# Sums of the FFN's down weights: from VectorE to accumulating transfers in DRAM

## The chip, the core and the metric

The kernel runs on one core of a Trainium2 chip. The core has five engines with queues of their own: TensorE (PE, matrix products, with its weight loads shown as PEld), VectorE (DVE), ScalarE (ACT), GpSimd (POOL) and SyncE (SP). Transfers between DRAM and on-chip memory are issued from the queues of SP, ACT and POOL and are carried out by 16 DMA engines that all queues share. The metric is the device time of one execution in microseconds (us); lower is better.

## The reference

The program computes two layers of a decoder trunk on 512 tokens of width 1024, in float32. Each layer normalises its input, projects it once into four parallel branches (a gated short convolution, a sparse attention with a top-k selection, a gated linear recurrence, a cross-attention into 256 memory tokens), lifts and gates the branches, sums them, projects and adds the residual. Then comes the feed-forward part (FFN), and only that is touched here:

```python
hf = rmsnorm(x, norm_ffn)
gate, up = jnp.split(hf @ ffn_w_up, 2, axis=-1)
return x + (jax.nn.silu(gate) * up) @ ffn_w_down      # ffn_w_down: 2816 x 1024 per layer
```

## The kernel before

Every product of float32 matrices is made of three products of rounded halves: an operand is split into `hi` and `lo`, and hi·hi, hi·lo and lo·hi are summed (`mm3`, lines 275 to 277). Weights come in through `wchunk` (line 219, on SP's queue) into one of two `w_raw` buffers of 1 MB; ACT writes the rounded half `w_hi` (through the helper at line 97) and DVE the rest `w_lo` (line 230), each into one of three buffers of half a chunk (`W_BUFS`).

A layer is first `mixer`, with the projections, the selection, the attention and the recurrence (`head`, whose first steps on DVE are the subtractions at line 911 and the scan at line 918, which reads `chunk_mult`, set by POOL at line 873), then `ffn`. In the middle of the mixer `values` makes the recurrence's values `hv` (line 688). The residual goes through a DRAM tensor, `x_spill`, written by eight stores at line 1030 and read again by POOL's transfers at line 1202 or 1207.

The FFN works in parts of four to six pairs of 128-row blocks of its hidden width. For each pair the up and gate products are made, then `operands` forms the left operands. The down product of a part is not made directly: `down` uses a scheme with seven block products in place of eight. With the weight block pair of index i cut into b11, b12, b21, b22 (row block first, column half second), it needs the sums

    t1 = b12 - b11,  t2 = b22 - t1,  t3 = b22 - b12,  t4 = b21 - t2

of the right operand, and like sums of the left one. `weight_sums` (lines 1084 to 1094) makes them one pair at a time: POOL loads 1 MB (line 1087), DVE makes four subtractions (lines 1090 to 1093), and POOL stores the four sums into the DRAM tensor `w_sums` (line 1094). The call for the next pair follows each pair's operands. `down` later loads them from there on SP's queue (lines 1151 and 1176). The loaded tile `w_raw7` of `weight_sums` is one buffer that the loads of `down` (every third of them, `raw_tile`) and of `x_in` use too. The last two pairs of layer 0 go without sums (`plain`, `add_down`). `evict` (line 1255) adds each finished product to the accumulator `acc`.

The order of the instructions on each engine is not that of the text. A planner (the framework's scheduler, which runs the program against its own model of times) takes for each engine, among the instructions whose inputs and buffers are free, the one of the highest priority, which is the earliest in the text if no priority is given. It puts in the semaphores, for on-chip tiles and for DRAM tensors. A manual dependency of kind NoSync only orders; one of kind Sync makes the instruction wait.

Of the kernel before, what the change touches and what calls it, by code (L numbers as in the profile page):

```python
# [12 lines left out]
F32 = mybir.dt.float32  # L13
# [4 lines left out]
OP = mybir.AluOpType  # L18
# [3 lines left out]
P = 128  # L22
# [47 lines left out]
def hybrid_trunk(ctx: ExitStack, tc: tile.TileContext, x, mem, positions, norm_mix, w_in, conv_w,  # L70
                 dsa_q_norm, dsa_k_norm, hgrn_lower_bounds, hgrn_out_norm, mem_norm, mem_w_kv,
                 mem_q_norm, mem_k_norm, w_lift, w_out, norm_ffn, ffn_w_up, ffn_w_down, out):
    nc = tc.nc
    act, dve, pe, pool = nc.scalar, nc.vector, nc.tensor, nc.gpsimd
# [8 lines left out]
    sp = start.enter_context(tc.tile_pool(name="start", bufs=1))  # L83

    order = mybir.DependencyInfo(mybir.DependencyClass.NoSync, mybir.DependencyReason.DATA)
    tables = {AF.Exp: "natural_log_exp_and_others", AF.Ln: "natural_log_exp_and_others",
              AF.Silu: "silu_and_others"}
    table = {"set": None, "load": None, "users": []}
# [14 lines left out]
    def mm_ps():  # L103
        return pmm.tile([P, 512], F32, name="mm")
# [4 lines left out]
    def tr_ps():  # L109
        return pat.tile([P, 512], F32, name="tr", bufs=TR_BUFS)  # L110

    def f(ap):
        return ap.bitcast(F32)
# [29 lines left out]
    ps = tr_ps()  # L143
    for _ in range(WARM):
        pe.matmul(ps[:, :P], ones_d, ones_d, start=True, stop=True)
    rows = sp.tile([P, P], F32, name="rows")
# [13 lines left out]
    ps = tr_ps()  # L160
# [80 lines left out]
    def wchunk(src, kt, n):  # L241
        return Chunk(src, kt, n)
# [19 lines left out]
    def tokens_wide(ws, a, kt, pss):  # L262

        k0 = 0
        for w in ws:
            for ks, _, _ in w.parts:
                for t, ps in enumerate(pss):
                    for k in ks:
                        mm3(ps, pair(a, k0 + k, slice(t * P, (t + 1) * P)), w.at(k), k0 + k == 0, k0 + k == kt - 1)
            k0 += w.kt  # L270
# [9 lines left out]
    wt_dram = nc.dram_tensor("w_sums", [DEPTH, P, FF // 256, 4, 512], F32, kind="Internal").ap()  # L280
    kv_dram = [nc.dram_tensor(f"kv{l}", [P, 4, 2, 2, MEM], F32, kind="Internal").ap() for l in range(DEPTH)]

    def new_h():
        return (state.tile([P, KD, S], F32R, name="h_hi", bufs=1),
                state.tile([P, KD, S], F32R, name="h_lo", bufs=1))
# [230 lines left out]
    def mixer(l, h, norms, cm):  # L516
# [165 lines left out]
        def values(hv):  # L682
            ws = [wchunk(w_in[l][k0 * P:(k0 + 4) * P, C_GI:C_GI + 512], 4, 512) for k0 in (0, 4)]
            pss = [mm_ps() for _ in range(MM_BUFS)] + [tr_ps()]
            tokens_wide(ws, h, KD, pss)
            for t, ps in enumerate(pss):
                with tc.high_priority(offset=AHEAD):
                    i = A(hv[:, t, :], ps, AF.Copy, scale=r_t[:, t:t + 1])
                if t < MM_BUFS:
                    behind.append(i)  # L690
            yield

        with pool_("dsa") as dp:
# [365 lines left out]
    HALF = S // 2  # L1059
    A11, A12, A22, S2, S1, S4, S3 = range(7)  # L1060
    C1, C2 = slice(512, 1024), slice(0, 512)
# [19 lines left out]

    SUM3, SUM1, SUM2, SUM4 = range(4)

    def weight_sums(fp, l, i):

        raw = fp.tile([P, 4, 512], F32, name="w_raw7")
        nc.gpsimd.dma_start(raw.rearrange("p (e c) n -> p e (c n)", e=2),
                            ffn_w_down[l][2 * i * P:2 * (i + 1) * P, :].rearrange("(e p) n -> p e n", p=P))
        b12, b11, b22, b21 = (raw[:, j, :] for j in range(4))
        dve.tensor_sub(b11, b12, b11)  # L1090
        dve.tensor_sub(b12, b22, b12)
        dve.tensor_sub(b22, b22, b11)
        dve.tensor_sub(b21, b21, b22)
        nc.gpsimd.dma_start(wt_dram[l, :, i], raw)

    def operands(fp, g0, g1, plain, n_ops):

        hi, lo = (fp.tile([P, 7, HALF], F32R, name=nm, bufs=n_ops) for nm in ("a_hi", "a_lo"))
        if plain:
            for o, g in ((0, g0), (2, g1)):  # L1100
                h_, l_ = (x[:, o:o + 2, :].rearrange("p a b -> p (a b)") for x in (hi, lo))
                A(h_, g, AF.Copy)
                dve.tensor_sub(l_, g, f(h_))
            return hi, lo

        def put(o, n, src):
            h_, l_ = (x[:, o:o + n, :].rearrange("p a b -> p (a b)") for x in (hi, lo))
            A(h_, src, AF.Copy)
            dve.tensor_sub(l_, src, f(h_))

        put(A11, 1, g0[:, :HALF])
        put(A12, 2, g1)
        dve.tensor_add(g0[:, HALF:], g0[:, HALF:], g1[:, HALF:])
        dve.tensor_sub(g0[:, :HALF], g0[:, HALF:], g0[:, :HALF])
        both = g1.rearrange("p (a b) -> p a b", b=HALF)
        dve.tensor_sub(both, both, g0[:, None, :HALF].to_broadcast([P, 2, HALF]))
        put(S2, 2, g0)
        put(S4, 2, g1)
        return hi, lo
# [73 lines left out]
    def ffn(l, h, ssq):  # L1193
        r_b = norm_feature(ssq)
        last = l == DEPTH - 1
        n_f = FF // 256
        parts = ((0, 6, False), (6, n_f, False)) if last else ((0, 5, False), (5, 9, False), (9, n_f, True))

        with tc.tile_pool(name="ffn", bufs=1, reuse_waits="tile") as fp:
            def x_chunk(m):  # L1200
                xc = fp.tile([P, S], F32, name="x_c", bufs=4)
                nc.gpsimd.dma_start(xc, x_dram[:, m, :])
                return xc

            def x_in(m0):
                xs = fp.tile([P, 2048], F32, name="w_raw7")
                nc.gpsimd.dma_start(xs.rearrange("p (m t) -> p m t", t=S), x_dram[:, m0:m0 + 4, :])
                for m in range(4):
                    ps = tr_ps()
                    for t in range(NT):  # L1210
                        pe.transpose(ps[:, t * P:(t + 1) * P], xs[:, m * S + t * P:m * S + (t + 1) * P], ident)
                    A(acc[:, :, (m0 + m) * P:(m0 + m + 1) * P], ps.rearrange("p (a b) -> p a b", b=P), AF.Copy)

            acc = None
            for part, (f0, f1, plain) in enumerate(parts):
                ops = []
                if not plain:
                    weight_sums(fp, l, f0)
                for fc in range(f0, f1):
                    wg = wchunk(ffn_w_up[l][:, fc * 256:(fc + 1) * 256], KD, 256)  # L1220
                    wu = wchunk(ffn_w_up[l][:, FF + fc * 256:FF + (fc + 1) * 256], KD, 256)
                    gs = [fp.tile([P, S], F32, name="fg", bufs=3) for _ in range(2)]
                    us = [fp.tile([P, S], F32, name="fu", bufs=2) for _ in range(2)]
                    for w, dsts in ((wg, gs), (wu, us)):
                        for dst, ps in zip(dsts, features(w, h, (0, 1))):
                            dve.tensor_mul(dst, ps, r_b)
                    for g, u in zip(gs, us):
                        A(g, g, AF.Silu)
                        dve.tensor_mul(g, g, u)  # L1229
                    ops.append(operands(fp, *gs, plain, 6 if last else 5))  # L1230
                    if acc is None:
                        acc = fp.tile([P, NT, D], F32, name="acc")
                        if not last:
                            pool.memset(acc, 0.0)
                    if last and fc in (1, 3):
                        x_in(2 * fc - 2)
                    if not plain and fc + 1 < f1:
                        weight_sums(fp, l, fc + 1)
                final = last and part == len(parts) - 1
                wd = ffn_w_down[l][f0 * 256:f1 * 256, :]  # L1240
                if plain:
                    h2, ssq2 = new_h(), new_ssq()
                    add_down(x_chunk, wd, [Pairs(t) for t in zip(*ops)], 2 * len(ops), acc, h2, ssq2,
                             lambda c: g_mix(l + 1, c))
                    return h2, ssq2

                def evict(bank, t0, cols, done=False, tail=False):
                    tail = final and tail
                    adds = []
                    with tc.high_priority(offset=2 * AHEAD):  # L1250
                        for t, ps in enumerate(bank):
                            for w in (slice(0, 256), slice(256, 512)) if tail else (slice(0, 512),):
                                c = slice(cols.start + w.start, cols.start + w.stop)
                                d = acc[:, t0 + t, c]
                                adds.append(dve.tensor_add(d, d, ps[:, w]))  # L1255
                                if final and done:
                                    q = nc.scalar if tail and w.start else nc.sync if t0 or tail else nc.gpsimd
                                    q.dma_start(out[0][(t0 + t) * P:(t0 + t + 1) * P, c], d)
                    return adds

                down(fp, wd, wt_dram[l, :, f0:f1], ops, evict)
        return None, None

# [33 lines left out]
```

## Time and profile before

| | |
|---|---|
| median of 3 runs | 2032.3 us (2030.45 to 2032.67) |
| the profiled execution | 2033.14 us, span 2031.4 us |
| PE busy | 2015.5 us, 99% of the span |
| DVE busy | 1427.8 us, 70% |
| ACT busy | 1067.9 us, 53% |
| POOL busy | 45.0 us, 2% |
| DMA queue of POOL | 46.80 MB, 6.2% of 16 engines' span |
| DMA queue of SP | 208.51 MB, 32.0% |

The profile is of one execution. In a row of instructions, `out<-in` names the tiles, then partitions x elements, a count, and times. A wait is put down to the instruction that ended it. PE's rows overlap, since matmuls are pipelined: a matmul of 512 columns is shown as 0.39 us, and starts 0.23 us after the one before it. `q1` is SP's DMA queue, `q0` POOL's, `q10` ACT's.

### The profile page before, as it was taken

What the parts mean: (1) busy time and instruction counts of PE and PEld (TensorE: products, weight loads), DVE (VectorE), ACT (ScalarE), POOL (GpSimd) and SP (SyncE); (2) the same over time, 40 slices, a digit from 0 to 9 for tenths busy, and PEclk for the clock granted to TensorE, in tenths of its full rate; (3) what the DMA queues carried; (4) which work ended last, traced back from release to release, by engine and by line L of the source; (5) the groups of instructions that cost most, each with busy time, mean ns of one, the idle gap of its engine ahead of it and who ended that gap; (6) DMA issues with size and microseconds to landing.
All of it is one profiled execution on the core that took longest, in us unless ns stands there. A gap on an engine that the chain in (4) does not pass through costs nothing.

```text
span 2031.4 us, 26667 instructions
## 1 busy us (share of the span) xinstructions
PE 2015.5 (99%) x10100; PEld 1691.8 (83%) x10100; DVE 1427.8 (70%) x2774; ACT 1067.9 (53%) x1914; POOL 45.0 (2%) x86
## 2 busy tenths in 40 slices
PE   9999999999999999999999999999999999999999
PEld 8998987778888888888889898877888788888887
DVE  5768897647776576666556889955678566666666
ACT  7653654766566433333345455477667544333333
POOL 0000000000000000000000000000000000000000
PEclk9999999999999999999999999999999999999999
DMA  7623232222233554663352223232222445566644
GB/s 252 214 88 104 68 104 62 78 69 83 83 110 123 196 213 150 227 232 128 108 182 71 92 79 94 73 94 67 80 79 80 152 140 192 186 212 217 225 150 155
DMA packets 192160, 269.86 MB, mean 133 GB/s; under 512 B 5775, under 2 KB 157921, under 8 KB 189089
## 3 DMA queue, kind: packets, MB, share of 16 engines
q1 hardware_dynamic: 176320, 208.51, 32.0%
q0 software_dynamic: 9568, 46.80, 6.2%
q10 hardware_dynamic: 6144, 12.87, 1.7%
q8 instruction: 79, 1.29, 0.3%
q14 instruction: 49, 0.39, 0.1%
HBM read 232.50 MB, written 35.65 MB: 132 GB/s over the span
## 4 chain that ended last, share of the span: by engine, by line
PE 95%; DVE 2%; DMA 2%; ACT 1%; issue 0%; DVEq 0%; SPq 0%; ACTq 0%
PE mm L275 28%; PE mm L277 27%; PE mm L276 27%; PE tr L732 1%; PE at L702 1%; PE tr L726 1%; PE at L703 1%; PE at L277 1%; PE at L276 1%; PE at L275 1%; DVE acc L1255 1%; PE tr L275 1%; PE tr L277 1%; PE tr L276 1%; DMA w_raw<-in_ffn_w_down_dram 1%; ACT w_hi L97 0%
## 5 line engine op out<-in xcount | busy, mean ns | idle before, releaser
L275 PE MATMUL mm<-h_hi,w_hi 128*128 128x512 f32 x1664 | 651.3, 393 | 1.4 <-ACT w_hi L97 0.7
L276 PE MATMUL mm<-h_lo,w_hi 128*128 128x512 f32 x1664 | 652.4, 392 | 0.0
L277 PE MATMUL mm<-h_hi,w_lo 128*128 128x512 f32 x1664 | 648.4, 392 | 0.6 <-DVE w_lo L230 0.5
L97 ACT ACTIVATE w_hi<-w_raw 128x1024 fp32r<-128x1024 f32 (+1 forms) x384 | 394.9, 1033 | 391.5 <-PE mm L276 248.5
L230 DVE TENSOR_TENSOR w_lo<-w_raw,w_hi 128x1024 fp32r<-128x1024 f32 x304 | 369.4, 1218 | 203.9 <-ACT w_hi L97 202.8
L275 PEld LDWEIGHTS mm<-h_hi,w_hi 128*128 128x128 f32 x1664 | 313.2, 188 | 67.2 <-ACT w_hi L97 1.8
L277 PEld LDWEIGHTS mm<-h_hi,w_lo 128*128 128x128 f32 x1664 | 312.8, 188 | 65.5 <-DVE w_lo L230 1.4
L276 PEld LDWEIGHTS mm<-h_lo,w_hi 128*128 128x128 f32 x1664 | 313.1, 188 | 63.8 <-issue 0.6
L1079 DVE TENSOR_TENSOR w_lo<-w_raw,w_hi 128x1024 fp32r<-128x1024 f32 (+1 forms) x80 | 86.4, 1090 | 64.9 <-ACT w_hi L97 64.8
L277 PE MATMUL mm<-w_hi,h_lo 128*128 128x256 f32 (+2 forms) x368 | 109.3, 297 | 0.0
L276 PE MATMUL mm<-w_lo,h_hi 128*128 128x256 f32 (+2 forms) x368 | 109.1, 297 | 0.0
L275 PE MATMUL mm<-w_hi,h_hi 128*128 128x256 f32 (+2 forms) x368 | 108.7, 298 | 0.0
L97 ACT ACTIVATE a_hi<-fg 128x512 fp32r<-128x512 f32 (+1 forms) x84 | 48.5, 580 | 109.1 <-DVE fg L1229 81.8
L275 PE MATMUL mm<-y_hi,w_hi 128*128 128x512 f32 x256 | 100.3, 394 | 1.2 <-ACT y_hi L97 1.2
L276 PE MATMUL mm<-y_lo,w_hi 128*128 128x512 f32 x256 | 100.5, 393 | 0.0
L277 PE MATMUL mm<-y_hi,w_lo 128*128 128x512 f32 x256 | 100.2, 392 | 0.0
L97 ACT ACTIVATE prob<-prob,small 128x256 f32<-128x256 f32 (+3 forms) x128 | 68.9, 555 | 16.7 <-DVE small L715 9.0
L276 PEld LDWEIGHTS mm<-w_lo,h_hi 128*128 128x128 f32 x368 | 70.1, 191 | 2.2
L277 PEld LDWEIGHTS mm<-w_hi,h_lo 128*128 128x128 f32 x368 | 70.0, 191 | 1.9
L275 PEld LDWEIGHTS mm<-w_hi,h_hi 128*128 128x128 f32 x368 | 69.8, 191 | 1.9
L97 ACT ACTIVATE gate_e<-gate 128x512 f32<-128x512 f32 x64 | 40.2, 628 | 45.2 <-DVE gate L534 44.6
L276 PE MATMUL mm<-w_lo,a_hi 128*128 128x512 f32 x160 | 62.2, 389 | 0.0
(404 smaller groups left out, 3301.3 us busy)
## 6 DMA issues: line engine op xcount, KB each, us to landing
w_raw<-in_w_in_dram SPq DMA_DIRECT2D x72, 1024.0 KB, 5.3
w_raw<-in_ffn_w_up_dram SPq DMA_DIRECT2D x44, 1024.0 KB, 5.3
w_raw<-in_ffn_w_down_dram POOLq DMA_DIRECT2D x20, 1024.0 KB, 5.7
w_sums<-w_raw POOLq DMA_DIRECT2D x20, 1024.0 KB, 4.5
w_raw<-in_w_lift_dram SPq DMA_DIRECT2D x32, 512.0 KB, 3.5
w_raw<-w_sums SPq DMA_DIRECT2D x20, 768.0 KB, 4.2
w_raw<-in_ffn_w_down_dram SPq DMA_DIRECT2D x9, 1024.0 KB, 6.1
w_raw<-in_mem_w_kv_dram SPq DMA_DIRECT2D x8, 1024.0 KB, 5.4
```

The costliest lines, as they stand in the source:

```text
L97: i = act.activation(dst, src, func, **kw)
L230: dve.tensor_sub(lo, raw[:, k:e], f(hi))
L275: return [pe.matmul(ps, ah, bh, start=first, stop=False, skip_group_check=more), pe.matmul(ps, ah, bl, start=False, stop=False, skip_group ...
L276: pe.matmul(ps, ah, bl, start=False, stop=False, skip_group_check=more),
L277: pe.matmul(ps, al, bh, start=False, stop=last, skip_group_check=more)]
L702: pe.matmul(ps, q[:, hh, s], k[0][:, :n], start=True, stop=False)
L703: pe.matmul(ps, q[:, hh, s], k[1][:, :n], start=False, stop=True)
L726: pe.transpose(pp[:, (2 * e + i) * P:(2 * e + i + 1) * P], probs[2 * i + e][:, b * P:(b + 1) * P], ident)
L732: pe.matmul(pv[e * HD:(e + 1) * HD, :], vt[:, b, :], pt[:, b, e * 2 * P:(e + 1) * 2 * P], start=b == 0, stop=b == t)
L1079: follow(dve.tensor_sub(lo[:, k:k + n, :], src, f(hi[:, k:k + n, :])), earlier)
L1255: adds.append(dve.tensor_add(d, d, ps[:, w]))
```

## The change

`weight_sums` is called once for each layer, at the end of `values`, and works in DRAM only. Four times it issues a copy from DRAM to DRAM on POOL's queue and then a transfer that adds another block to the copied one in place (`accum_op=OP.add`): t1 = b11 + b12, t2 = t1 + b22, t4 = t2 + b21, t3 = b12 + b22, in this order. Each transfer covers all eleven pairs of the layer (128 x 11 rows of 512 floats). The first copy of a layer waits for the last write of `hv`; no dependency is written for the others. The loads, the subtractions and the stores in the FFN go. Since the sums now carry other signs, `operands` forms its sums with other signs, two of them in a three-operand form (`scalar_tensor_tensor`), and `evict` subtracts for the columns C2 where it added.

```diff
--- before.py
+++ after.py
@@ -83,6 +83,7 @@
     sp = start.enter_context(tc.tile_pool(name="start", bufs=1))
 
     order = mybir.DependencyInfo(mybir.DependencyClass.NoSync, mybir.DependencyReason.DATA)
+    sync = mybir.DependencyInfo(mybir.DependencyClass.Sync, mybir.DependencyReason.DATA)
     tables = {AF.Exp: "natural_log_exp_and_others", AF.Ln: "natural_log_exp_and_others",
               AF.Silu: "silu_and_others"}
     table = {"set": None, "load": None, "users": []}
@@ -688,6 +689,7 @@
                     i = A(hv[:, t, :], ps, AF.Copy, scale=r_t[:, t:t + 1])
                 if t < MM_BUFS:
                     behind.append(i)
+            weight_sums(l, i)
             yield
 
         with pool_("dsa") as dp:
@@ -1081,17 +1083,17 @@
 
     SUM3, SUM1, SUM2, SUM4 = range(4)
 
-    def weight_sums(fp, l, i):
-
-        raw = fp.tile([P, 4, 512], F32, name="w_raw7")
-        nc.gpsimd.dma_start(raw.rearrange("p (e c) n -> p e (c n)", e=2),
-                            ffn_w_down[l][2 * i * P:2 * (i + 1) * P, :].rearrange("(e p) n -> p e n", p=P))
-        b12, b11, b22, b21 = (raw[:, j, :] for j in range(4))
-        dve.tensor_sub(b11, b12, b11)
-        dve.tensor_sub(b12, b22, b12)
-        dve.tensor_sub(b22, b22, b11)
-        dve.tensor_sub(b21, b21, b22)
-        nc.gpsimd.dma_start(wt_dram[l, :, i], raw)
+    def weight_sums(l, gate):
+
+        rows = ffn_w_down[l].rearrange("(i e p) n -> p i e n", e=2, p=P)
+        t3, t1, t2, t4 = (wt_dram[l, :, :, j] for j in range(4))
+        b11, b21, b12, b22 = (rows[:, :, e, c] for c in (C1, C2) for e in range(2))
+        for dst, src, more in ((t1, b11, b12), (t2, t1, b22), (t4, t2, b21), (t3, b12, b22)):
+            i = nc.gpsimd.dma_start(dst, src)
+            if gate is not None:
+                tc.add_manual_dep(i.ins, gate.ins.name, sync, reason="not sooner")
+                gate = None
+            nc.gpsimd.dma_start(dst, more, accum_op=OP.add)
 
     def operands(fp, g0, g1, plain, n_ops):
 
@@ -1110,10 +1112,12 @@
 
         put(A11, 1, g0[:, :HALF])
         put(A12, 2, g1)
-        dve.tensor_add(g0[:, HALF:], g0[:, HALF:], g1[:, HALF:])
-        dve.tensor_sub(g0[:, :HALF], g0[:, HALF:], g0[:, :HALF])
+        s2, s1 = g0[:, :HALF], g0[:, HALF:]
+        dve.tensor_sub(s1, g1[:, HALF:], s1)
+        dve.scalar_tensor_tensor(s2, s1, -1.0, s2, op0=OP.mult, op1=OP.subtract)
         both = g1.rearrange("p (a b) -> p a b", b=HALF)
-        dve.tensor_sub(both, both, g0[:, None, :HALF].to_broadcast([P, 2, HALF]))
+        dve.scalar_tensor_tensor(both, both, -1.0, s2[:, None, :].to_broadcast([P, 2, HALF]),
+                                 op0=OP.mult, op1=OP.subtract)
         put(S2, 2, g0)
         put(S4, 2, g1)
         return hi, lo
@@ -1214,8 +1218,6 @@
             acc = None
             for part, (f0, f1, plain) in enumerate(parts):
                 ops = []
-                if not plain:
-                    weight_sums(fp, l, f0)
                 for fc in range(f0, f1):
                     wg = wchunk(ffn_w_up[l][:, fc * 256:(fc + 1) * 256], KD, 256)
                     wu = wchunk(ffn_w_up[l][:, FF + fc * 256:FF + (fc + 1) * 256], KD, 256)
@@ -1234,8 +1236,6 @@
                             pool.memset(acc, 0.0)
                     if last and fc in (1, 3):
                         x_in(2 * fc - 2)
-                    if not plain and fc + 1 < f1:
-                        weight_sums(fp, l, fc + 1)
                 final = last and part == len(parts) - 1
                 wd = ffn_w_down[l][f0 * 256:f1 * 256, :]
                 if plain:
@@ -1252,7 +1252,7 @@
                             for w in (slice(0, 256), slice(256, 512)) if tail else (slice(0, 512),):
                                 c = slice(cols.start + w.start, cols.start + w.stop)
                                 d = acc[:, t0 + t, c]
-                                adds.append(dve.tensor_add(d, d, ps[:, w]))
+                                adds.append((dve.tensor_sub if cols is C2 else dve.tensor_add)(d, d, ps[:, w]))
                                 if final and done:
                                     q = nc.scalar if tail and w.start else nc.sync if t0 or tail else nc.gpsimd
                                     q.dma_start(out[0][(t0 + t) * P:(t0 + t + 1) * P, c], d)
```

## The prediction

> **What bounds the kernel now.** First the page: its span, its busiest engine and its DMA queues.
>
> ```profile
> span 2031.4 us, 26667 instructions
> ...
> PE 2015.5 (99%) x10100; PEld 1691.8 (83%) x10100; DVE 1427.8 (70%) x2774; ACT 1067.9 (53%) x1914; POOL 45.0 (2%) x86
> ...
> DMA packets 192160, 269.86 MB, mean 133 GB/s; under 512 B 5775, under 2 KB 157921, under 8 KB 189089
> ...
> q1 hardware_dynamic: 176320, 208.51, 32.0%
> q0 software_dynamic: 9568, 46.80, 6.2%
> q10 hardware_dynamic: 6144, 12.87, 1.7%
> ...
> w_raw<-in_w_in_dram SPq DMA_DIRECT2D x72, 1024.0 KB, 5.3
> ...
> w_sums<-w_raw POOLq DMA_DIRECT2D x20, 1024.0 KB, 4.5
> ```
>
> TensorE (PE) is idle for only 15.9 us, so nothing that frees another engine can bring more than that. The queue rows give rates with all 16 engines at work: q1 (weights, SP) 208.51 MB in 0.320 x 2031.4 us, 321 GB/s; q0 (POOL) 372 GB/s; q10 (stores) 373 GB/s. Most packets are under 2 KB: weights come in rows of 256 floats, 1 KB. A load of 1 MB lands 5.3 us after its issue. Next the windows by stage: length, then busy time of PE, PEld, DVE, ACT and POOL, PE's clock, the DMA engines' share, GB/s.
>
> ```profile
> 5.00:90.00 85.00, 80.98 (x594) 76.48 (x594) 58.51 (x187) 61.62 (x149) 1.26 (x5) 0.96 0.77 261
> 90.00:200.00 110.00, 109.38 (x662) 96.76 (x661) 85.25 (x274) 55.02 (x145) 0.20 (x2) 1.00 0.31 94
> 336.00:457.00 121.00, 119.14 (x591) 92.44 (x592) 65.97 (x162) 84.99 (x178) 1.49 (x4) 0.97 0.24 74
> 707.00:816.00 109.00, 108.82 (x480) 89.78 (x479) 74.70 (x106) 42.79 (x56) 5.59 (x9) 1.00 0.53 185
> 816.00:860.00 44.00, 43.51 (x192) 35.54 (x191) 30.97 (x39) 16.05 (x18) 1.79 (x3) 1.00 0.67 230
> 860.00:985.00 125.00, 124.93 (x551) 102.96 (x550) 83.57 (x112) 45.38 (x56) 3.25 (x6) 1.00 0.51 175
> ...
> 1687.00:1818.00 131.00, 130.81 (x593) 108.21 (x592) 87.18 (x123) 51.52 (x71) 7.91 (x13) 1.00 0.59 206
> 1818.00:1875.00 57.00, 56.28 (x248) 46.12 (x247) 38.88 (x47) 22.64 (x26) 1.26 (x2) 1.00 0.59 199
> 1875.00:1985.00 110.00, 110.00 (x487) 91.09 (x486) 71.08 (x100) 37.75 (x50) 5.03 (x8) 1.00 0.53 184
> ```
>
> The FFN windows (707 to 985, 1687 to 1985) hold a matmul every 227 ns (109.00 us / 480) and PE gaps of 0.18 + 0.49 + 0.07 + 0.19 + 0.72 + 0 = 1.65 us. The start, 5 to 90 us, is the one stage in which the DMA engines are loaded, 0.77; the mixer at 336 us uses 0.24 of them. Whether a load is late is read from ACT, which splits each loaded chunk (`w_hi`). First its whole-run wait for PE, then its groups within 5 to 90 us.
>
> ```profile
> ACT w_hi L97 <- PE mm L276: 248.5, 151, 5.2
> ```
>
> ```profile
> L97 ACT ACTIVATE w_hi<-w_raw 128x1024 fp32r<-128x1024 f32 x21 | 22.1, 1059 | 4.9 <-PE mm L277 2.4 <-DMA w_raw<-in_w_in_dram 1.3 <-DMA w_raw<-in_mem_w_kv_dram 1.2
> ```
>
> Over the run ACT waits for PE to free a `w_hi`, with the load long landed. In the start half of its wait (2.5 of 4.9 us) is for a load: there loads arrive just in time, and eight of 1 MB are issued in 43 us, one in 6.
>
> ```profile
> L219 SPq DMA_DIRECT2D w_raw<-in_mem_w_kv_dram x8: 367/368/603, 6.7 to 50.1; - x8
> ```
>
> **The change, part by part.** *Removed from the FFN*: 20 calls of `weight_sums`, each a load, four subtractions and a store.
>
> ```profile
> L1090 DVE TENSOR_TENSOR w_raw<-w_raw x20: 681/692/694, 704.9 to 1933.1; 128x512 f32<-128x512 f32 x20
> L1093 DVE TENSOR_TENSOR w_raw<-w_raw x20: 678/684/695, 707.0 to 1936.3; 128x512 f32<-128x512 f32 x20
> L1116 DVE TENSOR_TENSOR fg<-fg x20: 683/692/693, 726.2 to 1983.9; 128x512 f32<-128x512 f32 x20
> L601 DVE SCALAR_TENSOR_TENSOR gate<-gate,prm x8: 729/743/751, 163.1 to 1187.3; 128x512 f32<-128x512 f32 x8
> ```
>
> 80 x 0.688 = 55 us of DVE go, and 40 transfers of 1 MB (41.9 MB, 113 us at q0's rate). They lie beside a full PE; at most the 1.65 us of gaps can close, at least nothing. I take -1.5: no other tile is late behind them. *Signs*: two operations per block become three-operand forms, 0.743 against 0.692 us at 128x512, so 40 x 0.05 = 2 us more of DVE, under its 30% idle; add turned into subtract at the evictions costs nothing. Without that cover it would be +2.
>
> *Added*: per layer eight transfers on POOL's queue from DRAM to DRAM, each 128 x 11 x 512 floats = 2.88 MB: four copies, and four that add to what is there. They form two chains. t1, +, t2, +, t4, +: each reads what the one before wrote, and the first waits for the last `hv` (the gate). t3 and its addition: b12 is an input, nothing writes t3 earlier, and the gate is given to the first copy alone, so this pair waits for nothing. Where does it then go? POOL's own rows, one of ACT's stores and the scan on DVE:
>
> ```profile
> 4.76 0.32 POOL L139 TENSOR_SCALAR_AFFINE_SELECT tri_f<-tri_f 128x128 f32<-128x128 f32 x1
> 63.40 0.52 POOL L696 MEMSET k_lo<- 64x512 f32 x1 [58.33 <-DVE r L365]
> 87.45 0.52 POOL L743 MEMSET ik_lo<- 64x512 f32 x1 [23.52 <-DMA kv<-kv]
> ...
> 448.09 0.52 POOL L873 MEMSET chunk_mult<- 128x512 f32 x1 [278.25 <-PE tr L726]
> ...
> 667.55 0.56 POOL L1202 DMA_DIRECT2D x_c<-x_spill  x1 [5.85 <-DMA x_spill<-xT]
> ...
> 708.02 0.55 POOL L1094 DMA_DIRECT2D w_sums<-w_raw  x1 [26.08 <-DVE w_raw L1093]
> 712.74 0.72 POOL L1087 DMA_DIRECT2D w_raw<-in_ffn_w_down_dram  x1 [4.16 <-DMA w_sums<-w_raw]
> ```
>
> ```profile
> 335.05 0.69 ACT L97 ACTIVATE hv<-tr,rstd_t 128x512 f32<-128x512 f32 x1
> ```
>
> ```profile
> 698.15 0.33 ACTq L1030 DMA_DIRECT2D x_spill<-xT  x1
> ```
>
> ```profile
> 457.26 1.21 DVE L918 TENSOR_TENSOR_SCAN cum<-chunk_mult,ls 128x512 f32<-128x512 f32 x1
> ```
>
> The load of `x_c` belongs to the last part of the FFN, written far behind the sums' store of L1094, yet it stands 40 us ahead of it in POOL's queue, issued when its own slice of `x_spill` had landed and 31 us before the last slice was stored (698.15). So the planner puts what is ready first, however late it is written, and tracks DRAM by slices. By this both layers' t3 pairs go out when POOL falls idle, at 5 us, in the loaded start. Issuing is cheap: 0.55 us for a transfer of 128 rows (L1094), 0.72 for 256 (L1087), so some 2.3 us for 1408, of POOL's own idle time.
>
> *Price of a transfer.* No row shows DRAM to DRAM, nor an addition. A copy: 2.88 MB at 372 GB/s, 7.8 us, if its two sides overlap fully; read at q1's and written at q10's rate one after the other, 9.0 + 7.7 = 16.7 us. An addition: 7.8 us if its second read were free; two reads and a write, 25.7 us. I take 9.0 and 18.0, a load's rate and twice that, since the loads' packets (1 KB) are nearest in size to these 2 KB rows. [...]
>
> *t3 in the start.* Two copies and two additions: 54 us of all 16 engines (31 to 85 by the ends). The loads there have 0.77 x 85 = 65 us of work. If the two queues take turns, half each, both are slowed until the 54 us are done, at 5 + 108 = 113; the loads have then done 54 of 65 and need 11 more: 124 in place of 90, +34 us. By the ends: 31 gives +11; 85 makes the loads take 130, +45. PE has only 4 us of idle time there to give, so this is added to the span. POOL waits meanwhile with the memsets of 63 and 87 us behind the additions; the second addition is issued when both copies are in, at 5 + 36 = 41 us, so nothing is late.
>
> *The gated chain* starts at 335.7. POOL issues its sixth transfer when five have landed: 3 x 9 + 2 x 18 = 63 us, over 0.76 of the engines 83, plus some 1.7 us each for landing (a store of 1 MB lands in 4.5 against 2.8 us of movement) 91: at 427, before `chunk_mult` is wanted at 448. At the high prices: 103 / 0.76 + 8 = 143, at 479, 22 us after the scan of 457.3; DVE's weight splits stand behind that scan, and three `w_hi` (W_BUFS = 3), each good for 24 matmuls of 227 ns, cover 16 us: up to +6 per layer. I take 0. The loads there need 0.24 of the engines; at half turns a load of 5.3 us takes 11, hidden by ACT's waits for PE. The sums are wanted at 803.9, 270 us after the chain.
>
> ```profile
> L1151 SPq DMA_DIRECT2D w_raw<-w_sums x20: 319/320/339, 803.9 to 1996.4; - x20
> ```
>
> **Sum**, on the profiled execution's 2033.1 us (span 2031.4; 0.04% above the median of 2032.3): +34 - 1.5 = 2065.6, say 2066.
>
> **The rivals.** *Hidden* (not slower): the t3 pairs run only in gaps of the loads, 0.23 of 85 and 0.69 of 110 us, 95 us in all, which would hold 54; or the chip serves loads first. For it: additions are single, short bursts. Against it: loads there are just in time. 2031.6. It decides as long as a load of 5.3 us stays under the 6 us between loads there. *Turns by packet*: with 1 KB against 2 KB the loads get a third, not a half, of the engines. At my prices the t3 work then lasts 81 us, in which the loads do 27 of 65, and the other 38 bring them to 124 all the same; at the high prices it lasts 127 us, 42 are done, and 23 more end at 155: +65, 2096.6. For it: weights' packets are the smaller ones. [...] *The t3 pairs are not hoisted* and follow the gated chain: then POOL's memsets wait for seven landings, at my prices (90 / 0.76 + 12 = 130, at 466, 9 us late, covered: 2031.6), at the high ones (144 / 0.76 + 12 = 201, at 537, 80 us late, 64 lost per layer: 2160). Between them: 2070. *The freed DVE pays*: only if PE's gaps were more than the 1.65 us; faster than 2029 has no place in the windows but a luckier order in the start.
>
> **How the numbers follow.** The t3 pairs in the start at half turns: 0.44, own range 2042 to 2077 (+11 and +45, less 1.5). Turns by packet at the high prices: 0.18. Hidden: 0.15. Not hoisted: 0.17, a third of it without loss. Luck of the order: 0.06, faster. A difference under 0.2% (4 us) can hardly be told from none. Faster 0.06, same 0.20, slower 0.74. Range 2030 to 2098: it leaves out the unhoisted chain's high end, additions dearer than 25.7 us, and half the luck.
>
> **What would show it.** Right: POOL rows of `w_sums` near 5 us, DMA share near 1 from 5 to 120, ACT's `w_hi` waiting for `w_raw` loads by tens of us, PE at 227 ns in the FFN as before, no L1090 to L1093. Wrong: `w_sums` copies only after 335 us, or additions that land in less than 10 us, or a scan at L918 that waits for POOL.

## The result and the profile after

The changed kernel takes 2103.28 us in the median (2102.59 to 2105.17), against 2031.99 (2030.45 to 2032.67) before: a ratio of 1.0354, 95% interval 1.0341 to 1.0368, or 71.3 us more. The profiled execution took 2105.17 us, its span is 2103.4. The prediction of 2066 had the sign, but half the size, and the time lies 5 us beyond its range.

The page of the changed kernel: span, busy time, then by 40 slices of the span PE's granted clock and the share of the DMA engines, then the DMA queues.

```profile
span 2103.4 us, 26507 instructions
...
PE 2029.8 (96%) x10100; PEld 1702.2 (81%) x10100; DVE 1386.0 (66%) x2694; ACT 1069.4 (51%) x1914; POOL 41.4 (2%) x62
...
PEclk6799999999999999999999999999999999999999
DMA  9853223595224342442433322279522344336324
...
q1 hardware_dynamic: 176320, 208.51, 31.3%
q0 software_dynamic: 18400, 50.99, 10.4%
```

PE is idle for 73.6 us where it was for 15.9, and its clock is down in the first two slices. POOL's queue q0 moves hardly more bytes than before (50.99 against 46.80 MB), but its packets take 10.4% of the engines' time, before 6.2%: 219 us of all 16 engines for 16 transfers, at most 13.7 each (some 4.9 MB of other transfers are in it), where the prediction's 9.0 and 18.0 make 13.5 in the mean. The total price of the transfers was about right. POOL's timeline of the changed kernel (start, duration, idle time before and what ended it):

```profile
4.53 2.16 POOL L1092 DMA_DIRECT2D w_sums<-in_ffn_w_down_dram  x2
...
19.01 1.75 POOL L1096 DMA_DIRECT2D w_sums<-in_ffn_w_down_dram  x1 [11.76 <-DMA w_sums<-in_ffn_w_down_dram]
30.65 1.73 POOL L1096 DMA_DIRECT2D w_sums<-in_ffn_w_down_dram  x1 [9.89 <-DMA w_sums<-in_ffn_w_down_dram]
...
391.65 1.07 POOL L1092 DMA_DIRECT2D w_sums<-in_ffn_w_down_dram  x1 [167.62 <-ACT hv L98]
...
479.46 1.70 POOL L1096 DMA_DIRECT2D w_sums<-in_ffn_w_down_dram  x1 [15.21 <-DMA w_sums<-w_sums]
511.49 0.53 POOL L875 MEMSET chunk_mult<- 128x512 f32 x1 [30.34 <-PE tr L728]
```

The t3 copies of both layers stand at 4.53 us and their additions at 19 and 31, as forecast; the last of these lands at about 72 us. The gated chain runs from 391.65; `chunk_mult` waits for PE, not for the chain. Where the time goes is read from two rows of each layer: the last `hv`, and the accumulator's additions, whose first and last start bound the FFN. First the changed kernel, then the kernel before (its last `hv` starts at 335.1 and, in layer 1, at 1320.3):

```profile
L98 ACT ACTIVATE hv<-tr,rstd_t x2: 675/676/677, 390.7 to 1378.7; 128x512 f32<-128x512 f32 x2
...
L1255 DVE TENSOR_TENSOR acc<-acc,mm x40: 679/681/689, 878.8 to 2096.9; 128x512 f32<-128x512 f32 x40
```

```profile
L97 ACT ACTIVATE hv<-tr,rstd_t x2: 672/681/690, 335.1 to 1320.3; 128x512 f32<-128x512 f32 x2
...
L1255 DVE TENSOR_TENSOR acc<-acc,mm x40: 677/680/689, 820.0 to 2024.9; 128x512 f32<-128x512 f32 x40
```

The lag is 55.6 us at the first `hv`, 58.8 at the first `acc`, 58.4 at the second `hv` and 72.0 at the last `acc`: 56 us in the start, 3 in layer 0 behind `hv`, nothing in its FFN and the next layer's projections, 14 in layer 1. Of the stage between 860 and 985 us the changed kernel has the same row as before, 551 matmuls in 124.93 us:

```profile
860.00:985.00 125.00, 124.93 (x551) 103.00 (x550) 77.51 (x100) 46.53 (x57) 0.00 (x0) 1.00 0.42 137
```

Now the start. Windows of the changed kernel (length, then busy PE, PEld, DVE, ACT, POOL, PE's clock, DMA share, GB/s), then of the kernel before:

```profile
0.00:70.00 70.00, 30.71 (x161) 27.42 (x161) 13.83 (x49) 23.84 (x63) 9.68 (x17) 0.66 1.02 260
70.00:140.00 70.00, 59.87 (x408) 55.89 (x409) 46.23 (x142) 39.60 (x84) 1.19 (x4) 0.90 0.70 234
...
20.00:30.00 10.00, 0.00 (x0) 0.00 (x0) 0.00 (x0) 0.51 (x1) 0.76 (x1) 0.50 1.03 308
70.00:80.00 10.00, 5.71 (x30) 4.47 (x30) 6.20 (x14) 7.26 (x15) 0.00 (x0) 0.83 0.54 191
```

```profile
0.00:70.00 70.00, 64.90 (x484) 62.43 (x485) 46.21 (x139) 53.02 (x125) 4.57 (x14) 0.95 0.78 265
70.00:140.00 70.00, 69.34 (x454) 62.87 (x453) 47.54 (x185) 38.96 (x109) 0.66 (x3) 1.00 0.43 133
```

Busy time times clock is taken here as PE's work at full speed; up to 70 us it is 0.126 us for a matmul, and 0.127 before. Up to 70 us it is 30.71 x 0.66 = 20.3 against 64.90 x 0.95 = 61.7 us, 41 less; 34 of these are idle time, the rest is clock. From 70 to 140 it is 53.9 against 69.3, another 15 less, although the sums' traffic is over: 9.5 us of idle time, 6 of clock. Together 56.8, near the lag of 55.6 at `hv`. Between 20 and 30 us PE does nothing, and the clock is at 0.50; between 70 and 80 us it is 0.83, and between 860 and 985, where PE is full, 1.00. What PE waited for up to 70 us, and ACT up to 140, in the changed kernel (total, times, longest):

```profile
PE mm L276 <- ACT w_hi L98: 24.5, 2, 14.3
```

```profile
ACT w_hi L98 <- DMA w_raw<-in_mem_w_kv_dram: 26.2, 3, 14.4
```

### The profile page after: what moved, and what is told of

Read it like the earlier page. It is cut to its first block, busy times and chain, and to the rows that moved or that the text cites. A ratio compares the mean times of both kernels' runs of the same rounds, so it can differ in the third digit from the quotient of the medians.

```text
span 2103.4 us, 26507 instructions
## 1 busy us (share of the span) xinstructions
PE 2029.8 (96%) x10100; PEld 1702.2 (81%) x10100; DVE 1386.0 (66%) x2694; ACT 1069.4 (51%) x1914; POOL 41.4 (2%) x62
## 3 DMA queue, kind: packets, MB, share of 16 engines
q0 software_dynamic: 18400, 50.99, 10.4%
## 4 chain that ended last, share of the span: by engine, by line
PE 89%; DMA 6%; DVE 2%; ACT 2%; issue 0%; SPq 0%; DVEq 0%; ACTq 0%
PE mm L276 26%; PE mm L278 26%; PE mm L277 26%; DMA w_raw<-in_w_in_dram 4%; DMA w_raw<-in_mem_w_kv_dram 2%; PE at L278 1%; PE at L277 1%; PE at L276 1%; DVE w_lo L231 1%; PE at L704 1%; ACT w_hi L98 1%; PE at L705 1%; PE tr L734 1%; PE tr L728 1%; PE tr L278 1%; PE tr L277 1%
## 5 line engine op out<-in xcount | busy, mean ns | idle before, releaser
L276 PE MATMUL mm<-w_hi,mt_hi 128*128 128x256 f32 x128 | 40.5, 323 | 33.8 <-ACT w_hi L98 27.4
L1228 DVE TENSOR_TENSOR fg<-mm,rstd 128x512 f32<-128x512 f32 x44 | 30.2, 691 | 53.6 <-PE mm L278 53.5
## 6 DMA issues: line engine op xcount, KB each, us to landing
w_sums<-in_ffn_w_down_dram POOLq DMA_DIRECT2D x12, 2816.0 KB, 21.1
```

The costliest lines, as they stand in the source:

```text
L276: return [pe.matmul(ps, ah, bh, start=first, stop=False, skip_group_check=more), pe.matmul(ps, ah, bl, start=False, stop=False, skip_group ...
```

## The experiments

All times are medians. The kernel before took 2031.88 us beside the t3 pairs alone, their copies alone, the small rows and both chains gated; 2030.95 beside the pairs at another place, the chains alone, the t3 pairs of one block and the paced pieces; 2031.04 beside the 16 rows and the unpaced pieces. In the diffs, `-` is the changed kernel.

**The t3 pairs alone.** Only t3 is made, ungated; `down` loads it in place of the others.

```diff
-        for dst, src, more in ((t1, b11, b12), (t2, t1, b22), (t4, t2, b21), (t3, b12, b22)):
+        for dst, src, more in ((t3, b12, b22),):
...
-            nc.sync.dma_start(raw, sums[:, i, SUM1:])
+            nc.sync.dma_start(raw, sums[:, i, SUM3:SUM3 + 1].to_broadcast([P, 3, 512]))
```

> Only the t3 pairs are made, ungated, in the start; t1, t2, t4 and their chain are left out, and the down product loads t3 three times in their place, so the result is not the reference's. Theory A: 2031 + 56 = 2087 (2080 to 2092), with the start as in the changed kernel. Rival (the start recovers, and what is lost is lost in the mixer): under 2060.

2078.01 us, +46.1, 2 us under the first theory's range. **And without their additions**, against that kernel:

```diff
-            nc.gpsimd.dma_start(dst, more, accum_op=OP.add)
```

> As the run with the t3 pairs alone, but without their additions: two copies in the start and nothing else; b12 stands in place of the sums. If the cost goes by the time in which the traffic holds the engines (copies until 31 us, additions until 70 us), 2031 + 20 = 2051 (2045 to 2060). If the copies alone do the harm by hitting the first loads, 2075 to 2087. If only additions are slow on the engines, under 2040.

2054.59 us, +22.7. So 5.8 MB of copies cost 23 us and two additions as much again. The prediction's way of counting (traffic less the gaps of the loads) said +34 for the pairs and was short by a quarter. For the copies alone it says nothing at all: their 18 us fit into the 20 us that the loads leave free (0.23 of 85), and at half turns the loads would be done at 88 us, before the 90 of the kernel before. So what failed is not the price of the traffic but the belief that the loads can make up in the gaps what they lost.

**Who gets the engines.** Packets, MB and share of 16 engines of both queues in the changed kernel, while both are full: first the copies (15 to 31 us), then the additions (35 to 70 us).

```profile
q0 software_dynamic: 945, 3.57, 74.2%
q1 hardware_dynamic: 947, 1.29, 27.0%
...
q0 software_dynamic: 2525, 5.13, 78.8%
q1 hardware_dynamic: 2569, 3.25, 31.5%
```

The queues move packets in like number, 945 to 947 and 2525 to 2569, as they would by the rival's turns by packet. But packets are unlike: the copies' hold 3.8 KB in the mean and take 0.742 x 256 us / 945 = 0.20 us, the additions' 2.0 KB and 0.17 us, the loads' 1.3 KB and 0.07 us. So the loads keep 27 to 31% of the engines, neither half nor a third. Would smaller rows even this out?

```diff
-            i = nc.gpsimd.dma_start(dst, src)
...
+            for w in (slice(0, 256), slice(256, 512)):
+                i = nc.gpsimd.dma_start(dst[:, :, w], src[:, :, w])
...
-            nc.gpsimd.dma_start(dst, more, accum_op=OP.add)
+            for w in (slice(0, 256), slice(256, 512)):
+                nc.gpsimd.dma_start(dst[:, :, w], more[:, :, w], accum_op=OP.add)
```

> Every transfer of the chains is made as two, each of half the columns, so that its rows are 1 KB as the weights' and not 2 KB; the work and the gate stay. If the engines take turns by packet, the loads get about half in place of 21 to 34%, the start costs some 30 us in place of 56, and the whole is 2070 to 2082. If they take turns by bytes or by what is outstanding, no change or a little worse: 2098 to 2115.

2105.38 us, no change, as the second theory had it, though not for its reason. In this kernel the copies (15 to 31 us), then the additions (35 to 50 us):

```profile
q0 software_dynamic: 1013, 3.62, 69.6%
q1 hardware_dynamic: 1019, 1.73, 31.5%
...
q0 software_dynamic: 1703, 1.73, 71.1%
q1 hardware_dynamic: 1703, 1.91, 45.1%
```

A copy's packets hold 3.6 KB in the mean, hardly less than before, though its rows have 1 KB; only the additions' packets follow the rows (1.0 KB). So the edit did not change what it was to change in the copies. In the additions it did: the packets are equal in number, 1703 to 1703, and the loads have 45% of the engines, about the half of the first theory. (From 35 to 70 us q0 moved 4368 packets and q1 3153, but there q1 at times had hardly a load to move: 7 packets to 427 between 65 and 68 us.) The last `hv` came 8.8 us sooner (381.9 against 390.7) and the time was lost again behind it.

**The same pairs at another place.** As the kernel with the t3 pairs alone, but both layers' pairs wait for layer 0's last `iw`, in a stage where the loads of the kernel before take 0.31 of the engines (142 to 200 us).

```diff
+                    if l == 0 and t == NT - 1:
+                        weight_sums(0, i)
+                        weight_sums(1, i)
```

> The t3 pairs of both layers alone, as in the kernel with these pairs only (t1, t2, t4 left out, the FFN's loads take t3 in their place), but gated on layer 0's last iw (142 us), where the loads need 0.19 to 0.31 of the engines. Theory (backlogged loads keep 27 to 31%, so it costs what they need above that): 2031 to 2042, with some w_hi late by 5 to 12 us. Rival (the same bytes cost the same wherever they run): 2070 to 2085.

2036.54 us, ratio to before 1.0025 (1.0016 to 1.0034): +5.6 in place of +46. The bytes are the same, the place decides. (The start also keeps the order of the kernel before; what an order costs is tested below.) Between 142 and 200 us the loads get 24% of the engines, of the 31% they took before, and four of them come late by 15.5 us together:

```profile
q0 software_dynamic: 3134, 9.20, 62.9%
q1 hardware_dynamic: 3764, 3.92, 24.0%
```

```profile
ACT w_hi L98 <- DMA w_raw<-in_w_in_dram: 15.5, 4, 8.2
```

**The gated chains alone.** t3 is left out (its slot is filled from t1's in the load).

```diff
-        for dst, src, more in ((t1, b11, b12), (t2, t1, b22), (t4, t2, b21), (t3, b12, b22)):
+        for dst, src, more in ((t1, b11, b12), (t2, t1, b22), (t4, t2, b21)):
...
-            nc.sync.dma_start(raw[:, 0::2, :], sums[:, i0:i0 + m, SUM3])
+            nc.sync.dma_start(raw[:, 0::2, :], sums[:, i0:i0 + m, SUM1])
```

> The gated chains of t1, t2 and t4 alone: the t3 pairs are left out (the FFN's loads take the t1 slot in their place), so the start holds no copies. Theory (the three costs of the change add up: start, gated chain of layer 0, gated chain of layer 1): what is left of +71 after the t3 pairs alone (+46) is some +25, and the milestones of the changed kernel give the chains +17; so 2046 to 2060, hv of layer 0 at 335 as before, a stall of PE of some 6 us around the first copy of each layer. Rival (the chains cost only because the late start had pushed the loads together): 2030 to 2036.

2045.90 us, ratio 1.0071 (1.0056 to 1.0086): +15.0, just under the lower end. The chains cost by themselves; the prediction had +0. By the rows of `hv` and `acc` the profiled execution lost 2.4 us in layer 0 and 10.9 in layer 1. Why layer 1 more: POOL's first copy of layer 1, the next load that SP issues, ACT's split of it, and what DVE then waited for, in this kernel:

```profile
1321.30 1.06 POOL L1092 DMA_DIRECT2D w_sums<-in_ffn_w_down_dram  x1 [167.45 <-ACT hv L98]
...
1322.20 0.37 SPq L220 DMA_DIRECT2D w_raw<-in_w_in_dram  x1
...
1338.37 1.06 ACT L98 ACTIVATE w_hi<-w_raw 128x1024 fp32r<-128x1024 f32 x1 [13.41 <-DMA w_raw<-in_w_in_dram]
```

```profile
DVE w_lo L231 <- ACT w_hi L98: 40.6, 17, 15.8
```

The split of the same load in the kernel before:

```profile
1327.39 1.06 ACT L97 ACTIVATE w_hi<-w_raw 128x1024 fp32r<-128x1024 f32 x1 [2.44 <-DMA w_raw<-in_w_in_dram]
```

The load is issued 0.9 us behind the copy and lands 16 us later in place of 5. It was just in time before, with ACT already waiting 2.44 us for it. DVE stands 15.8 us at the `w_lo` of this chunk, with the attention's steps behind it, and PE waits for one of those (PE's waits in layer 1 of the chains alone):

```profile
PE at L704 <- DVE small L717: 10.1, 4, 7.2
```

In layer 0 the longest wait for a load is 6.1 us.

**Both chains with t3 in them.** The gate is given to t1's and to t3's first copy, so that the start is clean.

```diff
-            if gate is not None:
+            if dst is t1 or dst is t3:
                 tc.add_manual_dep(i.ins, gate.ins.name, sync, reason="not sooner")
-                gate = None
```

> The t3 copies get the gate too, so that all eight transfers of a layer start after its values; nothing is left out. Theory A (the ungated t3 pairs in the start cost about 56 us, the gated chains about 15): the first 100 us look as before the change (PE over 90 us busy), the time falls to 2045 to 2060, since the chain in the mixer is longer by one copy and one addition. Rival B (the cost goes with the traffic, wherever it runs): 2095 to 2105, with the PE gaps moved into the mixer. Rival C (POOL's memsets come late behind eight transfers): the scan on DVE waits for chunk_mult and the time is 2060 to 2090.

2062.17 us, ratio 1.0156 (1.0139 to 1.0174): the start's loss is gone (`hv` at 334.0), and the two chains cost +30 in place of +15. POOL sets `chunk_mult` at 456.88 behind PE, so the fear that the scan would wait for POOL was unfounded. The time is 2 us above the first theory's range and within the third's, but the third's mechanism is not there: it was the late loads again, up to 17.7 us in layer 1.

**The 15 us after the traffic: order or loads?** The planner puts ACT, DVE and PE in another order in the start as soon as POOL has transfers there. The next two kernels keep t3's transfers at their place, but cut them to one block in eleven, and to 16 rows of that block (the FFN loads t1's slot in t3's place).

```diff
+            if dst is t3:
+                dst, src, more = (a[:, :1] for a in (dst, src, more))
             i = nc.gpsimd.dma_start(dst, src)
```

> The changed kernel with the t3 pairs cut to one block of eleven (0.26 MB a transfer in place of 2.88), still ungated; t1, t2, t4 as they are; the FFN's loads take the t1 slot in t3's place, the other ten blocks of t3 are left out. In the start ACT, DVE and PE then issue in an order as far from the kernel before as the changed kernel's, with a tenth of the traffic. If the 15 us that the start lost after the traffic had ended come from that order: the chain-only kernel's time + 8 to 15. If they come from loads and clock: the chain-only kernel's time + 0 to 5 (5 us of traffic at 28%).

2056.29 us, 10.4 above the chain alone: this looked like the order. But the loss stands where the traffic is. Windows of this kernel, then of the chain alone:

```profile
10.00:20.00 10.00, 7.03 (x28) 5.63 (x29) 6.02 (x16) 6.58 (x14) 0.35 (x1) 0.51 1.04 335
20.00:30.00 10.00, 7.93 (x50) 7.33 (x49) 3.08 (x5) 8.15 (x24) 0.00 (x0) 0.84 0.69 223
```

```profile
10.00:20.00 10.00, 9.02 (x47) 7.58 (x48) 5.82 (x14) 9.16 (x18) 0.00 (x0) 0.66 1.06 381
20.00:30.00 10.00, 9.66 (x81) 9.46 (x80) 6.96 (x14) 8.43 (x26) 0.00 (x0) 1.00 0.62 207
```

50 matmuls fewer in these 20 us. By busy time times clock that is 10.3 in place of 15.6 us of PE's work, about half of the 10.4; the rest is lost behind `hv` (107.4 in place of 111.7 us between 320 and 440 us). The second kernel takes the bytes away (diff against the first):

```diff
-                dst, src, more = (a[:, :1] for a in (dst, src, more))
+                dst, src, more = (a[:16, :1] for a in (dst, src, more))
```

> As the kernel with tiny t3 pairs, but of each t3 transfer only 16 rows of one block, 32 KB (the rest of t3 is left out and the FFN's loads take the t1 slot in its place): the planner's order in the start stays about as far from before's as the changed kernel's, and almost nothing is moved there. If the tiny pairs' +10 over the chain-only kernel came from that order: 2053 to 2059. If it came from their 1 MB among the first loads (PE's clock and the first chunks between 10 and 30 us): 2043 to 2049, as with the chain alone.

2046.39 us, ratio 1.0077 (1.0062 to 1.0092), 0.5 above the chain alone. So the +10 came from 1 MB among the first loads, and an order about as far from before's costs next to nothing. The order of the changed kernel itself was not run without its traffic.

**Small pieces, not paced.** Each transfer is cut into its blocks of 256 KB; all wait for the last `hv` alone. Layer 0's two pairs without sums are left out.

```diff
+        for i in range(9 if l == 0 else FF // 256):
+            t3, t1, t2, t4 = (wt_dram[l, :, i, j] for j in range(4))
...
+                d = nc.gpsimd.dma_start(dst, src)
+                tc.add_manual_dep(d.ins, gate.ins.name, sync, reason="not sooner")
+                nc.gpsimd.dma_start(dst, more, accum_op=OP.add)
```

> The sums in pieces of 256 KB as in the paced kernel (72 and 88 transfers, nothing left out of the computation), but all of a layer's copies gated on the last hv alone, so that the planner puts what is ready in a row: up to 15 copies one behind the other. Theory (the backlog counts, not the size of a transfer): a load issued beside the first copies is late by some 10 us, as in the kernel with the chain alone; 2036 to 2056. Rival (small transfers let the loads through by themselves): 2029 to 2035.

2069.91 us, ratio 1.0189 (1.0172 to 1.0206): worse than the theory had it. The range had been taken from the chain without t3; beside the chain with t3 (2062) it is 8 us more. POOL issues up to nine copies in 4.78 us, the queues move packets in like number again (1203 to 1220), and the first load is as late as with large transfers. Queues of this kernel between 343 and 358 us, and ACT's wait:

```profile
q0 software_dynamic: 1203, 3.32, 76.0%
q1 hardware_dynamic: 1220, 1.23, 28.7%
```

```profile
359.12 1.06 ACT L98 ACTIVATE w_hi<-w_raw 128x1024 fp32r<-128x1024 f32 x1 [14.54 <-DMA w_raw<-in_w_in_dram]
```

**Small pieces, paced.** The same pieces, kept in a list; behind the last `hv`, each half of a chunk that is split issues one, which waits for its `w_lo`.

```diff
-                    dve.tensor_sub(lo, raw[:, k:e], f(hi))
+                    gate = dve.tensor_sub(lo, raw[:, k:e], f(hi))
+                one_piece(gate)
...
+    def one_piece(gate):
+        if pending:
+            dst, src, kw = pending.pop(0)
+            i = nc.gpsimd.dma_start(dst, src, **kw)
+            tc.add_manual_dep(i.ins, gate.ins.name, sync, reason="not sooner")
```

> The same sums in 72 and 88 small transfers of 256 KB (one block of 128 x 512), t3 among them, each gated on the split of one more loaded chunk behind the last hv, so about one in 5 to 6 us, on into the FFN; layer 0's two blocks that no sum needs are not made; nothing of the computation is left out. Theory (what costs is a backlog on both queues, in which the loads keep 27 to 31% of the engines; the bytes as such are free beside loads that need 0.24 to 0.6): 2028 to 2038, PE's idle time 14 to 22 us, no wait of w_hi for a load of over 10 us. Rival (DRAM-to-DRAM traffic costs wherever it runs, by its bytes): 2060 to 2100.

2030.73 us, ratio to before 0.9996 (0.9986 to 1.0006). POOL's queue on the page of this kernel, and the split of the load that was late in the chain:

```profile
q0 software_dynamic: 19168, 46.81, 10.3%
```

```profile
1327.72 1.06 ACT L98 ACTIVATE w_hi<-w_raw 128x1024 fp32r<-128x1024 f32 x1 [3.23 <-DMA w_raw<-in_w_in_dram]
```

q0 takes 10.3% of the engines, as in the changed kernel, and costs nothing. Little of it is under way at a time: in the median the pieces made from the weights land 5.2 us behind their issue and those made from `w_sums` 3.0, and they are issued 6.1 us apart in layer 0 and 6.7 in layer 1. This also draws layer 0's pieces out over 431 us in place of 83; the two cannot be had apart. Nor does it bring anything: DVE's freed 45 us stay hidden behind PE.

| kernel | us | lag at `hv` 0 | at first `acc` | at `hv` 1 | at last `acc` |
|---|---|---|---|---|---|
| changed | 2103.28 | 55.6 | 58.8 | 58.4 | 72.0 |
| t3 pairs alone | 2078.01 | 53.7 | 46.1 | 45.8 | 44.6 |
| t3 copies alone | 2054.59 | 28.8 | 21.3 | 21.1 | 20.0 |
| chains alone | 2045.90 | -2.0 | 0.4 | 0.0 | 10.9 |
| all gated | 2062.17 | -1.1 | 8.3 | 8.2 | 28.9 |
| paced | 2030.73 | -0.8 | -0.3 | -0.4 | -1.4 |

The lags are those of the profiled executions. The parts do not quite add up: 46.1 + 15.0 = 61 of 71 us. The table shows where: the two kernels with t3 alone win back 7.5 us between `hv` and the first `acc`, and the changed kernel, whose chain runs there, loses 3. PE behind the last `hv` of layer 0, in the kernel before, with the t3 pairs alone, and in the changed kernel:

```profile
336.00:346.00 10.00, 8.14 (x27) 6.78 (x28) 6.56 (x22) 6.07 (x18) 0.00 (x0) 0.66 0.26 77
```

```profile
386.00:396.00 10.00, 9.66 (x47) 7.86 (x46) 4.84 (x18) 7.52 (x21) 0.00 (x0) 1.00 0.43 132
```

```profile
405.00:415.00 10.00, 4.19 (x14) 2.83 (x15) 3.91 (x10) 5.48 (x12) 1.69 (x1) 0.67 0.92 195
```

The kernel before has a pause here: PE waits 2.9 us for a step of DVE, and its clock is 0.66 in the mean of this window. With t3 alone the pause is gone, by busy time times clock 9.7 in place of 5.4 us of work; that is most of the 7.5, and why DVE is in time there was not followed. The changed kernel has lost this pause too, but then stands again, because a split of ACT waits 12.3 us for its load. So its chain costs some 11 us in layer 0 (7.5 and 3), and 46 + 11 + 14 make the 71. The chains alone still have the pause, and cost only 2.4 us there; that the late load hides in it is argued from this, not shown.

## Why the prediction was wrong

*The hoist*: right, to the microsecond (4.53 against 5), with both layers' pairs. *The FFN*: full at the same rate as before, and the removed work was worth nothing there, as forecast within 1.5 us. *The signs*: no cost seen, the paced kernel carries them too; the three-operand form took 0.692 us at 128x512, as the two-operand form did, and not 0.743. *POOL's memsets*: on time.

*Prices of the transfers*: about right. In the changed kernel q0 took 51.6% of the engines between 391 and 408 us for the first copy behind `hv`, 8.8 us of all 16 where 9.0 were assumed, and 81.9% between 480 and 500 us for the third addition of that chain, 16.4 where 18.0 were assumed. In latency, in the kernel with the chains alone, the step from copy to addition took 13.6 us and from addition to the next copy 22.4; with its 0.76 of the engines and 1.7 us of landing the prediction had 13.5 and 25.4. The sixth transfer came 85.5 us behind the first, forecast was 91:

```profile
334.12 1.07 POOL L1092 DMA_DIRECT2D w_sums<-in_ffn_w_down_dram  x1 [166.10 <-ACT hv L98]
347.76 1.76 POOL L1096 DMA_DIRECT2D w_sums<-in_ffn_w_down_dram  x1 [12.58 <-DMA w_sums<-in_ffn_w_down_dram]
370.14 0.88 POOL L1092 DMA_DIRECT2D w_sums<-w_sums  x1 [20.62 <-DMA w_sums<-in_ffn_w_down_dram]
```

That an addition takes twice a copy's time was the author's estimate: by the engines' time it took 1.9 times as long here (16.4 against 8.8 us), by the steps of the chain 1.6 times (22.4 against 13.6).

*t3 in the start, the step that failed.* The prediction let the loads run at half turns beside 54 us of traffic and "have then done 54 of 65 and need 11 more: 124 in place of 90". The share was nearer 28%. That alone would have moved little: as the rival had worked out, at these prices the loads would end at 124 by either share, if they ran at full rate as soon as the traffic ended. They did not. Loads go through two `w_raw` buffers, which are free again when DVE has made `w_lo`, and the engines stood at 0.54 right behind the traffic and at 0.70 from 70 to 140 us. In these 70 us SP's queue waited 60.8 us for DVE before it could issue a load, and 0.4 us for another load. The two longest of these waits:

```profile
SPq L220 <- DVE w_lo L231: 42.6, 5, 11.9
SPq L220 <- DVE kv L479: 11.6, 2, 6.5
```

So the loads were held back by the work on the chunks before, not by the engines. PE, nearly full in this stage before (69.34 of 70 us), had nothing to catch up with, and it came back with a lower clock (0.90 from 70 to 140 us, where it was 1.00) and behind dry buffers. So 41 us were lost beside the traffic and 15 behind it: +56 in place of +34, and +46 at the end of the run with the t3 pairs alone, since the pause behind `hv` is won back. The tiny t3 pairs show how dear the first loads are: 1 MB between them cost 10 us in the end, 5 of them at once. The place as the cause is shown by the same pairs at 142 us (+5.6); that the 15 us come from loads and clock together rests on the windows and on the order's innocence in a like kernel, and how much is each was not separated.

*The gated chain, +0, the other step that failed*: "at half turns a load of 5.3 us takes 11, hidden by ACT's waits for PE". The load took 16, and the cover was read from a total over the whole run (248.5 us of waits for PE). In that very place of layer 1 ACT waits for the load already in the kernel before (2.44 us). The chains alone cost +15, and by the lags some 25 in the changed kernel.

*The rivals.* Turns by packet is what the counts agree with (945 to 947, 2525 to 2569), and was held to cost more only at high prices. "Hidden" is what the paced kernel shows to be possible, not in the start but behind `hv`; its loads from `in_w_in` landed 5.7 us behind their issue in the median of the run, 5.3 before.

## What to carry to other kernels

A low mean DMA share did not make background transfers free (10.4% of the engines for q0, +71 us): while both queues were full they moved packets in like number, and the one whose packets took 0.17 to 0.20 us had 74 to 79% of the engines, the loads with 0.07 us 27 to 31%. So keep the background queue short by gating each small piece on a step of the foreground (here one piece per half of a loaded chunk: +0; the same pieces without the pacing: +39). Look at the stage, not the run, for the cover of a late load, and count no catching up where the busiest engine is already full (here 41 us were lost beside the traffic and 15 more behind it). A dependency on the first of several transfers did not hold the others: what was ready went out first, however late it is written (t3's copies at 4.53 us).

## What was not expected

The copies from DRAM to DRAM moved packets of 4.0 KB in the mean with rows of 2 KB (720 packets for the 2.88 MB of the first copy behind `hv` in the changed kernel, 391 to 408 us) and with rows of 1 KB (543 for 2.16 MB between 7 and 15 us); the means of 3.6 and 3.8 KB above are of windows with a few shorter ones. The accumulating transfers' packets followed their rows, 2.0 and 1.0 KB. SP's own issuing took longer too: the two loads of `xin` in the start take 6.40 us to issue in the changed kernel, against 1.08 with the chains alone.
